# First-layer small TensorE work moved along a handwritten order, in a two-layer encoder kernel

## The chip, the cores and the metric

The kernel runs on one core of a Trainium2 chip. The metric is the device time of one execution, in microseconds (us). TensorE (PE in the profile) multiplies matrices, with its weight loads shown apart as PEld; VectorE (DVE), ScalarE (ACT) and GpSimd (POOL) work beside it, and DMA engines move data between the device memory and the core, at the order of the queues of SP and POOL.

## The reference

The input x has 256 rows of 2048 numbers, all float32. Two layers are computed on it, then a last norm.

```
layer 0:  hn = rmsnorm(x);  q,k,v,u,za,zb = split(hn @ w_in)         (2048 x 6144)
          o_a = chunked_attention(q,k,v, 16 heads x 64) * silu(za)
          y   = gelu(s5(u));  o_b = y * sigmoid(y @ w_glu + b_glu) * silu(zb)
          x   = x + concat(o_a, o_b) @ w_out
layer 1:  q,k,v,z,f = split(rmsnorm(x) @ w_in)                        (2048 x 8208)
          x   = x + (forgetting_attention(q,k,v,f, 16 heads x 128) * silu(z)) @ w_out
out = rmsnorm(x)
```

`s5` is a linear recurrence. For each of 64 channel groups a complex state of 64 numbers follows `x_t = A x_(t-1) + B u_t` over the 256 rows, with A diagonal, and `y_t = Re(C x_t) + D u_t` is read from it.

## The kernel before

**Projections.** All large products go through `project` (L168). A product is cut into column blocks of 512, and a block into chunks: a chunk is one weight tile of 128 x 1024 (512 KB, two blocks of 128 rows). `next_w` (L148) loads the tile into `wr` (4 buffers, issued on SP) and splits it into a high part `wh` on ScalarE and a low part `wl` on VectorE (3 buffers each), so that three matmuls of a reduced format give the product's precision. A chunk is 12 matmuls: two row halves, two blocks, three products of parts. The splits have a priority 3000 instructions ahead of their place.

**A clock of chunks.** The order of TensorE's instructions is the order in which the program writes them (`manual_schedule` for PE, L54); the order on the other engines and the DMA queues comes from a scheduler that simulates the program. Small work on TensorE is put between chunks by hand: `at_chunk(c, task)` queues a generator, `tick` runs after each chunk and resumes what is due, and `yield n` in a task lets n chunks pass. So the text below names a place by the number of chunks ahead of it: u is chunks 0 to 15, za of the first half 16 to 23, then q, k, v, and again za, q, k, v of the second half to 79, zb 80 to 95, the output product of the attention branch `oa0` to `oa3` 96 to 111, GLU 112 to 119, the output product of the other branch `oe0` to `oe3` 120 to 135; layer 1 follows. The host lays the weights in the same order (`_lay`, L1032), since `next_w` takes tile after tile.

**The recurrence (mixer B)** is cut into steps of 8 rows. Its parts, as tasks:
- `setup_task` (L722) prepares powers of A from chunk 3 on, `tables(e, ...)` (L343) then works for one of 8 sets of 8 groups: DVE makes `w1` and `mx`; after GAPS[e] chunks TensorE transposes `w1` (pm, L389) and multiplies `bb` and `mx` to lag tables (pk, L395), which go to device memory as `k_d` (four writes on SP, L402). Then it spawns the next set's `tables`, and at chunk READY[e], at the earliest two chunks on, multiplies u by the table (pv, L414); two chunks later it transposes the result (pvt, L425), and ScalarE copies it into `X`.
- `u_in` (L434) loads u back from device memory in another layout (`un`, L439), spreads it with four ScalarE copies (L445) and transposes it on TensorE (pu, L454) into `uT`, the operand of pv and of the lag products.
- `s5_tail` (L641) is spawned by the last set's pk. It loads the lag tables T0 to T6 with eight DMAs each on POOL's queue (`load_T`, L629) into space that the tables' working tiles have left, into 7 buffers; multiplies u by them (`products`, pyi, L656), one set of 16 small matmuls per table, and after each set loads T7 (after the first) or one of the tiles `mo` into the freed buffer. `scan_task` (L473) runs the recurrence over 30 steps of four DVE instructions. At chunk S5_OUT the second products (py) read `X` and `mo`. Then `yn` goes to device memory, is transposed to `yT` (pyt, L690), the operand of GLU, and read back as `y`, which POOL multiplies into `zb` (L707).

**Attention of layer 0.** `pair` (L577) loads the bias tile `bt` (SP), sets a corner of it on POOL, transposes q and k of two heads (pqk), one chunk later computes scores (psc), and four chunks later transposes the probabilities; `mixes` multiply them by v. The list at L750 says at which chunk each starts.

**GLU** (L780) writes `ob`; `glu_out` transposes it two chunks after each half (po_b, L558), and ScalarE and DVE write the parts `bTh`, `bTl`, the operands of `oe`. In layer 1 `forget` (L823) computes the log gates `lf` on DVE, and TensorE sums them (pc, L875) six chunks later.

Of the kernel before, what the change touches and what calls it, by code (L numbers as in the profile page):

```python
# [11 lines left out]
AF = mybir.ActivationFunctionType  # L12
# [7 lines left out]
D = 2048  # L20
# [7 lines left out]
G, GC, PS5 = 64, 16, 64  # L28
# [8 lines left out]
MAGIC = 12582912.0  # L37
PI_F = 3.1415925
SPLIT_AHEAD = 3000
SCAN_SLOW, S5_OUT = 78, 94  # L40


@with_exitstack
def trunk(ctx: ExitStack, tc: tile.TileContext, a, out: bass.AP):
# [74 lines left out]
    def at_chunk(c, task):  # L119

        seq[0] += 1
        queue.append((c, seq[0], task))
        if not busy:
            run_due()
# [18 lines left out]
        run_due()  # L143


    wpos = [0]

    def next_w(split=None, dst=None):  # L148
        i = wpos[0]
        wpos[0] += 1  # L150
        raw = wp.tile([P, CK * NT], F32, name=f"wr_{i}", tag="wr", bufs=4)
        if dst:
            wh, wl = dst
        else:
            wh = wp.tile([P, CK * NT], F32R, name=f"wh_{i}", tag="wh", bufs=3)
            wl = wp.tile([P, CK * NT], F32R, name=f"wl_{i}", tag="wl", bufs=3)
        step = NT if split else CK * NT
        for o in range(0, CK * NT, step):
            c = slice(o, o + step)
            nc.sync.dma_start(raw[:, c], a["w"][i][:, c])  # L160
            if split:
                split(o // NT)
            with tc.high_priority(offset=SPLIT_AHEAD):
                nc.scalar.activation(wh[:, c], raw[:, c], AF.Copy)  # L164
                nc.vector.tensor_tensor(wl[:, c], raw[:, c], wh[:, c].bitcast(F32), op=ALU.subtract)  # L165
        return wh, wl

# [259 lines left out]
            nc.scalar.copy(X[:, 1:, w, e * 8:e * 8 + 8],  # L427
                           pt[:, w].rearrange("p k (g n) -> p n (k g)", n=NCH))

    GAPS, READY = (9, 6, 6, 6, 6, 6, 7, 7), (24, 0, 0, 0, 0, 0, 0, 0)  # L430
    uT = s5b.tile([P, NGQ, P], F32, name="uT")
    un = X = None

    def u_in():  # L434

        nonlocal un, X
        un = res.tile([P, TC, G * GC // 4], F32, name="un", tag="X")
        for g4 in range(4):
            nc.sync.dma_start(un[32 * g4:32 * g4 + 32],  # L439
                              u_d[:, g4 * 256:(g4 + 1) * 256].rearrange("(n j) f -> n j f", j=TC))  # L440
        un4s = []

        def spread(b):
            un4 = s5b.tile([P, 4, TC, GC], F32, name=f"un4_{b}", tag="vs", bufs=2)
            nc.scalar.copy(un4, un[:, ::-1, b * 64:(b + 1) * 64].rearrange("p j (k c) -> p k j c", c=GC))  # L445
            un4s.append(un4)

        spread(0)
        spread(1)
        yield 3  # L450
        for b in range(4):
            pu = ps_s.tile([P, 4, P], F32, name=f"pu_{b}", tag="s")
            for k in range(4):
                nc.tensor.transpose(pu[:, k, :], un4s[b][:, k].rearrange("p j c -> p (j c)"), ident)  # L454
            nc.scalar.copy(uT[:, b * 4:b * 4 + 4, :], pu)
            if b < 2:
                spread(b + 2)
            if b == 1:
                yield 1
        X = res.tile([P, NCH + 1, 2, G], F32, name="X", tag="X")  # L460
        nc.gpsimd.memset(X[:, 0], 0.0)
# [103 lines left out]
    class Half:  # L565
# [11 lines left out]
        def pair(self, hp):  # L577

            hf = self.hf
            h0 = hf * 8 + hp * 2  # L580
            bt = at.tile([P, 2, L], F32, name=f"bt_{hf}_{hp}", tag="bt")
            nc.sync.dma_start(bt, bass.AP(rbx.tensor, rbx.offset + h0 * 384, [[1, P], [384, 2], [1, L]]))
            nc.gpsimd.memset(bt[0:64, :, 0:64], NEG)
            pqk = ps_s.tile([P, 2, L], F32, name=f"pqk_{hf}_{hp}", tag="s")
            for w, src in ((0, self.q), (1, self.k)):
                for t in range(2):
                    nc.tensor.transpose(pqk[:, w, t * P:(t + 1) * P], src[:, t, hp * P:(hp + 1) * P], ident)
            qkT = at.tile([P, 2, L], F32, name=f"qkT_{hf}_{hp}", tag="qkT")
            nc.scalar.copy(qkT, pqk)
            yield 1  # L590
            pscs = scores(qkT[:, 0, :], qkT[:, 1, :], [slice(0, 64), slice(64, 128)], [f"a{h0}", f"a{h0 + 1}"])
            lgs = [probs(at, pscs[hh], bt[:, hh, P - 1::-1], bt[:, hh, ::-1], f"a{h0 + hh}", scaled=True)
                   for hh in range(2)]
            yield 4
            for hh in range(2):
                self.work.append(turn_probs(at, lgs[hh], f"a{h0 + hh}", scaled=True))
# [44 lines left out]
    def s5_tail():  # L641
# [18 lines left out]
        tabs, mos = [load_T(e) for e in range(7)], []  # L660
        yield 5
        at_chunk(clock[0], scan_task())
        for e in range(8):
            pi_ = products(e, "pyi", lambda gq, g4: uT[:, gq, 32 * g4:32 * g4 + 32], tabs[e])
            nc.scalar.copy(y_of(e), pi_)
            if e == 0:
                tabs.append(load_T(7))
            else:
                mos.append(load_mo(e - 1))
            if e % 2:  # L670
                yield 2 if e < 5 else 4
        yield S5_OUT - clock[0]
        for e in range(8):
            py = products(e, "py", lambda gq, g4: X[:, 0:NCH, 0, gq * 4 + g4], mos[e])
            V.tensor_tensor(y_of(e), py, y_of(e), op=ALU.add)
# [38 lines left out]
    def load_xas(*ns):  # L714
        for n in ns:
            load_xa(n)
        yield None
# [29 lines left out]
    project(xTh, xTl, 16, "u1", u1_out, pre)  # L747
    at_chunk(clock[0], u_in())

    for c, task in ((41, a0.pair(0)), (45, a0.pair(1)), (49, a0.mixes(0)), (49, a0.pair(2)), (52, a0.mixes(1)),  # L750
                    (53, a0.pair(3)), (56, a0.mixes(2)), (60, a0.mixes(3)),
                    (73, a1.pair(0)), (77, a1.pair(1)), (81, a1.mixes(0)), (81, a1.pair(2)), (84, a1.mixes(1)),
                    (85, a1.pair(3)), (88, a1.mixes(2)), (92, a1.mixes(3)), (93, load_xas(0, 1, 2)), (96, load_xas(3))):
        at_chunk(c, task)
    zb = []
    a0.zaT = gate_T(0)
# [10 lines left out]
        project(xTh, xTl, 16, f"zb{n}", silu(z_))  # L767


    for n in range(4):  # L770
        project(aTh, aTl, 8, f"oa{n}",
                lambda t, acc: V.tensor_tensor(xa[n][:, t, :], acc, xa[n][:, t, :], op=ALU.add))


    def glu_out(n, ob):
# [4 lines left out]
    for n in range(2):  # L780
# [9 lines left out]
        project(yT[:, 0], yT[:, 1], 8, f"glu{n}", evac)  # L790
        at_chunk(clock[0], glu_out(n, ob))

    x = res.tile([P, 2, D], F32, name="xr", tag="X")
    x1Th = actp.tile([P, 16, L], F32R, name="x1Th", tag="ah")
    x1Tl = actp.tile([P, 16, L], F32R, name="x1Tl", tag="al")
# [27 lines left out]
    def forget():  # L823
# [45 lines left out]
        nc.vector.tensor_tensor(fe, fe, lf2, op=ALU.mult)  # L869
        nc.vector.scalar_tensor_tensor(fl, fe, -1.0, fl, op0=ALU.add, op1=ALU.add)  # L870
        nc.vector.scalar_tensor_tensor(lf2, fx2, 0.0, fl, op0=ALU.min, op1=ALU.subtract)
        yield 6
        pc = ps_s.tile([P, 2, CH], F32, name="pc", tag="s")
        U = tri[:, P:2 * P]
        nc.tensor.matmul(pc[:, 0, :], U, lf[:, 0, :], start=True, stop=True)  # L875
# [156 lines left out]
def _lay(inputs):  # L1032
    import numpy as np

    f = {k: np.asarray(v) for k, v in inputs.items()}

    def tiles(w, n0, n1):

        w = w[:, n0 * NT:n1 * NT]
        K, N = w.shape  # L1040
        w = w.reshape(K // (CK * P), CK, P, N // NT, NT).transpose(3, 0, 2, 1, 4)
        return w.reshape(-1, P, CK * NT)

    we, wo = f["w_in_even"][0], f["w_in_odd"][0]
    q, k, v, u, za, zb = 0, 2, 4, 6, 8, 10
    order = [u, u + 1, za, q, k, v, za + 1, q + 1, k + 1, v + 1, zb, zb + 1]
    parts = [tiles(we, n, n + 1) for n in order]
    wout = f["w_out_even"][0]
    parts += [tiles(wout[:D // 2], 0, 4), tiles(f["w_glu"][0], 0, 2), tiles(wout[D // 2:], 0, 4)]
    for g in range(4):  # L1050
        parts += [tiles(wo, n, n + 1) for n in (g, 4 + g, 8 + g, 12 + g)]
    parts.append(tiles(f["w_out_odd"][0], 0, 4))

    perm = np.array([(s % 4) * NGQ + s // 4 for s in range(G)])

    def lanes(re, im):
        return np.concatenate([re, im], 0)

    bre, bim = (f[n][0].transpose(1, 0, 2)[:, perm] for n in ("s5_b_re", "s5_b_im"))
    cre, cim = (f[n][0].transpose(2, 0, 1)[:, perm] for n in ("s5_c_re", "s5_c_im"))  # L1060
    bc = np.stack([lanes(bre, bim), lanes(bim, bre), lanes(cre, cim), lanes(cim, cre)], 2)
    d = f["s5_d"][0].reshape(4, NGQ, GC).transpose(0, 2, 1)
    dpad = np.zeros((4, 32, NGQ), d.dtype)
    dpad[:, :GC] = d
    rb = f["rel_bias"][0]
    ext = np.concatenate([rb[:, 1:], np.repeat(rb[:, 256:], 128, 1)], 1)
    return {
        "x": f["x"][0],
        "xT": f["x"][0].T.reshape(16, P, L).transpose(1, 0, 2),
        "w": np.concatenate(parts, 0),  # L1070
        "wf": wo[:, 4 * D:].reshape(16, P, CH).transpose(1, 0, 2).reshape(P, 16 * CH),
        "gE": f["norm_even_g"][0].reshape(16, P).T,
        "gO": f["norm_odd_g"][0].reshape(16, P).T,
        "gF": f["final_norm_g"].reshape(1, D),
        "rbx": ext,
        "bglu": f["b_glu"],
        "bf": f["b_forget"],
        "s5lr": f["s5_lambda_re"][0][perm].T,
        "s5li": f["s5_lambda_im"][0][perm].T,
        "s5dt": f["s5_log_dt"][0][perm].reshape(1, G),  # L1080
        "s5d": dpad.reshape(P, NGQ),
        "s5bc": bc,
    }
# [22 lines left out]
```

## Time and profile before

| what | us |
|---|---|
| median of 3 runs (lowest to highest) | 977.43 (976.41 to 978.26) |
| the profiled execution | 977.11 |
| its span, first to last instruction | 975.4 |
| TensorE busy | 935.1 (96%) |
| VectorE busy | 581.9 (60%) |
| ScalarE busy | 513.5 (53%) |
| GpSimd busy | 104.7 (11%) |
| mean granted TensorE clock | 0.985 |

A row of the list of waits names the waiting engine, its tile and line, who ended the wait, then the time in all, the number of waits and the longest. A row of the timeline has the start and the length of an instruction or of a few alike, the engine, line, operation, out<-in, shapes and count, and in brackets the idle time ahead of it and what ended that. Matmuls overlap in the pipeline, so the time of one is read from start to start, not from its length. A row of windows has the stretch, its length, the busy time and count of PE, PEld, DVE, ACT and POOL, then the granted clock, the DMA share and GB/s. A row of groups has count, then busy time and mean nanoseconds.

### The profile page before, as it was taken

Reading aid. Unit: us, or ns where it says so; the run is one execution under the profiler, and the core shown is the slowest. Engines: PE = TensorE matmul, PEld = TensorE weight load, DVE = VectorE, ACT = ScalarE, POOL = GpSimd, SP = SyncE. Lnnn points to the kernel's source line nnn. Section 1 sums busy time; section 2 is a strip of 40 time slices with the busy share of each in tenths; the row PEclk is TensorE's granted clock in tenths of the full one; section 3 lists DMA queues with packets and bytes.
Section 4 is the critical chain, followed back from the end, with each engine's and each line's share of the span. In section 5 each row is a group of like instructions: output and inputs, shape, how many; then the busy total and the mean of one; then the engine's idle time right before and its main releaser. Section 6 shows DMA issues by size and latency. Waiting matters only on the chain.

```text
span 975.4 us, 13235 instructions
## 1 busy us (share of the span) xinstructions
PE 935.1 (96%) x4814; PEld 759.9 (78%) x4814; DVE 581.9 (60%) x1023; ACT 513.5 (53%) x815; POOL 104.7 (11%) x177
## 2 busy tenths in 40 slices
PE   7969999999689999999999999999999999999996
PEld 5848777777567778887887888888888888888884
DVE  7885777774885446666655545454545454545563
ACT  6636546684246765355544644464446544644451
POOL 2000000001760000200001400040004000200200
PEclk9988999999899999999999999999999999999998
DMA  9885566646988577754556554546564545455562
GB/s 326 288 236 184 189 187 204 203 147 206 198 216 293 177 232 224 230 183 161 173 200 215 174 194 159 195 166 194 171 195 140 199 160 193 153 192 166 192 202 87
DMA packets 68546, 190.43 MB, mean 195 GB/s; under 512 B 7936, under 2 KB 22512, under 8 KB 68096
## 3 DMA queue, kind: packets, MB, share of 16 engines
q1 hardware_dynamic: 65056, 181.07, 56.9%
q0 software_dynamic: 3424, 8.51, 3.8%
q8 instruction: 38, 0.62, 0.3%
q14 instruction: 28, 0.23, 0.1%
HBM read 180.09 MB, written 9.45 MB: 194 GB/s over the span
## 4 chain that ended last, share of the span: by engine, by line
PE 82%; DMA 5%; DVE 5%; issue 3%; ACT 2%; POOL 1%; SPq 1%; POOLq 0%; DVEq 0%; ACTq 0%
PE acc_cq L175 3%; PE acc_cv L177 3%; PE acc_cv L176 3%; PE acc_cz L175 3%; PE acc_cq L177 3%; PE acc_cv L175 3%; PE acc_cq L176 3%; PE acc_cz L177 3%; PE acc_cz L176 3%; PE acc_ck L175 3%; PE acc_ck L176 3%; PE acc_ck L177 3%; PE acc_oo L177 3%; PE acc_oo L175 3%; PE acc_oo L176 3%
## 5 line engine op out<-in xcount | busy, mean ns | idle before, releaser
L165 DVE TENSOR_TENSOR wl<-wr,wh 128x1024 fp32r<-128x1024 f32 (+1 forms) x292 | 360.9, 1236 | 290.2 <-ACT wh L164 289.6
L164 ACT ACTIVATE wh<-wr 128x1024 fp32r<-128x1024 f32 (+1 forms) x292 | 309.7, 1061 | 341.3 <-PE acc_cz L177 46.7
L175 PE MATMUL acc_cv<-wh,x1Th 128*128 128x512 f32 x128 | 51.3, 400 | 0.0
L175 PE MATMUL acc_cq<-wh,x1Th 128*128 128x512 f32 x128 | 50.6, 395 | 0.0
L175 PE MATMUL acc_cz<-wh,x1Th 128*128 128x512 f32 x128 | 50.2, 392 | 0.0
L177 PE MATMUL acc_cv<-wh,x1Tl 128*128 128x512 f32 x128 | 50.0, 390 | 0.0
L175 PE MATMUL acc_ck<-wh,x1Th 128*128 128x512 f32 x128 | 49.9, 390 | 0.0
L176 PE MATMUL acc_cv<-wl,x1Th 128*128 128x512 f32 x128 | 49.9, 390 | 0.0
L177 PE MATMUL acc_cq<-wh,x1Tl 128*128 128x512 f32 x128 | 49.9, 390 | 0.0
L176 PE MATMUL acc_cq<-wl,x1Th 128*128 128x512 f32 x128 | 49.8, 389 | 0.0
L177 PE MATMUL acc_cz<-wh,x1Tl 128*128 128x512 f32 x128 | 49.8, 389 | 0.0
L177 PE MATMUL acc_ck<-wh,x1Tl 128*128 128x512 f32 x128 | 49.8, 389 | 0.0
L176 PE MATMUL acc_ck<-wl,x1Th 128*128 128x512 f32 x128 | 49.8, 389 | 0.0
L176 PE MATMUL acc_cz<-wl,x1Th 128*128 128x512 f32 x128 | 49.8, 389 | 0.0
L910 POOL TENSOR_SCALAR cbt<-ckb,cum 128x128 f32<-128x128 f32 x16 | 13.5, 844 | 309.6 <-DVE mx_c L527 265.4
L175 PE MATMUL acc_oo<-wh,oTh 128*128 128x512 f32 x108 | 42.2, 391 | 0.0
L177 PE MATMUL acc_oo<-wh,oTl 128*128 128x512 f32 x108 | 42.0, 389 | 0.0
L176 PE MATMUL acc_oo<-wl,oTh 128*128 128x512 f32 x108 | 42.0, 389 | 0.0
L633 POOL DMA_DIRECT2D T<-k_d x64 | 33.5, 532 | 41.8 <-DMA k_d<-ks 32.9
L175 PE MATMUL acc_u<-wh,xTh 128*128 128x512 f32 x64 | 26.0, 407 | 6.1 <-ACT wh L164 6.1
L175 PEld LDWEIGHTS acc_ck<-wh,x1Th 128*128 128x128 f32 x128 | 24.0, 188 | 5.4 <-issue 0.4
L177 PEld LDWEIGHTS acc_cq<-wh,x1Tl 128*128 128x128 f32 x128 | 24.0, 188 | 5.1
(407 smaller groups left out, 2084.4 us busy)
## 6 DMA issues: line engine op xcount, KB each, us to landing
wr<-in_w_dram SPq DMA_DIRECT2D x295, 512.0 KB, 3.4
m_d<-mx SPq DMA_DIRECT2D x8, 512.0 KB, 5.4
T<-k_d POOLq DMA_DIRECT2D x64, 64.0 KB, 4.7
mo<-m_d POOLq DMA_DIRECT2D x8, 512.0 KB, 8.2
bt<-in_rbx_dram SPq DMA_DIRECT2D x8, 256.0 KB, 6.2
bc<-in_s5bc_dram SPq DMA_DIRECT2D x8, 256.0 KB, 4.0
xt<-in_x_dram SPq DMA_DIRECT2D x2, 1024.0 KB, 7.8
xa<-in_x_dram SPq DMA_DIRECT2D x4, 512.0 KB, 5.7
```

What stands on the lines that cost most here:

```text
L164: nc.scalar.activation(wh[:, c], raw[:, c], AF.Copy)
L165: nc.vector.tensor_tensor(wl[:, c], raw[:, c], wh[:, c].bitcast(F32), op=ALU.subtract)
L175: nc.tensor.matmul(acc[t], sh, wh[:, c], start=kb == 0, stop=False)
L176: nc.tensor.matmul(acc[t], sh, wl[:, c], start=False, stop=False)
L177: nc.tensor.matmul(acc[t], sl, wh[:, c], start=False, stop=kb == nkb - 1)
L633: nc.gpsimd.dma_start(tt_[j * GC:(j + 1) * GC], k_d[e, :, :, GC * (j + 1):GC * (j + 1) + P])
L910: W.tensor_scalar(bt[:, 0, :], self.ckb[:, hh, 0:P], cum[:, 0, h:h + 1], None, op0=ALU.add)
```

## The change

No computation changes; instructions and the order of weight tiles move.

- The first table's pm and pk come 12 chunks after its DVE work was started instead of 9 (chunk 22 instead of 19), pv of it at chunk 28 instead of 24; the gaps of the last two tables are 6 instead of 7, so the last pm and pk come at chunk 64 instead of 63.
- `u_in` still issues the load of `un` at chunk 16, but spreads at 23 instead of 16 and transposes at 25 and 26 instead of 19 and 20. Each spread copy is tied behind the last `wh` split that the program has written by then (`issue_after` orders instructions of one engine).
- The lag products come one table at a time at chunks 71, 74, ... 92, instead of two at 68, 70, 72 and 76. The scan starts at 69 instead of 68 and changes its pace at 79 instead of 78; the second products start at 95 instead of 94.
- A pair's `bt` load and its memset are written two chunks ahead of its transposes; these stay at their chunks.
- GLU is computed ahead of `oa3` instead of behind it: chunks 108 to 115, with `oa3` at 116 to 119.
- In layer 1 pc comes seven chunks after the gates' DVE work instead of six.

```diff
-SCAN_SLOW, S5_OUT = 78, 94
+SCAN_SLOW, S5_OUT = 79, 95
...
-                nc.scalar.activation(wh[:, c], raw[:, c], AF.Copy)
+                last_split[:] = [nc.scalar.activation(wh[:, c], raw[:, c], AF.Copy)]
...
-    GAPS, READY = (9, 6, 6, 6, 6, 6, 7, 7), (24, 0, 0, 0, 0, 0, 0, 0)
+    GAPS, READY = (12, 6, 6, 6, 6, 6, 6, 6), (28, 0, 0, 0, 0, 0, 0, 0)
...
-            nc.scalar.copy(un4, un[:, ::-1, b * 64:(b + 1) * 64].rearrange("p j (k c) -> p k j c", c=GC))
+            with tc.issue_after(last_split[0].ins):
+                nc.scalar.copy(un4, un[:, ::-1, b * 64:(b + 1) * 64].rearrange("p j (k c) -> p k j c", c=GC))
             un4s.append(un4)
 
+        yield 7
         spread(0)
         spread(1)
-        yield 3
+        yield 2
...
             nc.gpsimd.memset(bt[0:64, :, 0:64], NEG)
+            yield 2
             pqk = ps_s.tile([P, 2, L], F32, name=f"pqk_{hf}_{hp}", tag="s")
...
         yield 5
         at_chunk(clock[0], scan_task())
+        yield 2
         for e in range(8):
...
-            if e % 2:
-                yield 2 if e < 5 else 4
-        yield S5_OUT - clock[0]
+            yield 3 if e < 7 else S5_OUT - clock[0]
...
-    for c, task in ((41, a0.pair(0)), (45, a0.pair(1)), (49, a0.mixes(0)), (49, a0.pair(2)), (52, a0.mixes(1)),
-                    (53, a0.pair(3)), (56, a0.mixes(2)), (60, a0.mixes(3)),
-                    (73, a1.pair(0)), (77, a1.pair(1)), (81, a1.mixes(0)), (81, a1.pair(2)), (84, a1.mixes(1)),
-                    (85, a1.pair(3)), (88, a1.mixes(2)), (92, a1.mixes(3)), (93, load_xas(0, 1, 2)), (96, load_xas(3))):
+    for c, task in ((39, a0.pair(0)), (43, a0.pair(1)), (49, a0.mixes(0)), (47, a0.pair(2)), (52, a0.mixes(1)),
+                    (51, a0.pair(3)), (56, a0.mixes(2)), (60, a0.mixes(3)),
+                    (71, a1.pair(0)), (75, a1.pair(1)), (81, a1.mixes(0)), (79, a1.pair(2)), (84, a1.mixes(1)),
+                    (83, a1.pair(3)), (88, a1.mixes(2)), (92, a1.mixes(3)), (93, load_xas(0, 1, 2)), (96, load_xas(3))):
...
-    for n in range(4):
+    def out_a(n):
         project(aTh, aTl, 8, f"oa{n}",
                 lambda t, acc: V.tensor_tensor(xa[n][:, t, :], acc, xa[n][:, t, :], op=ALU.add))
+
+    for n in range(3):
+        out_a(n)
...
         at_chunk(clock[0], glu_out(n, ob))
 
+    out_a(3)
...
-        yield 6
+        yield 7
         pc = ps_s.tile([P, 2, CH], F32, name="pc", tag="s")
...
-    parts += [tiles(wout[:D // 2], 0, 4), tiles(f["w_glu"][0], 0, 2), tiles(wout[D // 2:], 0, 4)]
+    parts += [tiles(wout[:D // 2], 0, 3), tiles(f["w_glu"][0], 0, 2), tiles(wout[:D // 2], 3, 4),
+              tiles(wout[D // 2:], 0, 4)]
```

More of the change, by code (lines that the diff above doesn't have):

```diff
@@ L143, in tick @@
         run_due()
-    wpos = [0]
+    wpos, last_split = [0], []
     def next_w(split=None, dst=None):
```

## The prediction, made before the changed kernel was run

> **What bounds the kernel now.** I read the list of waits on TensorE first, then TensorE's instructions in time around each long wait, then the other engines and DMA there.
>
> ```profile
> span 975.4 us, 13235 instructions
> ```
>
> ```profile
> PE pyi L656 <- DMA T<-k_d: 11.0, 3, 6.5
> ...
> PE pu L454 <- ACT un L445: 4.9, 1, 4.9
> PE pk L395 <- DVE mx L380: 4.0, 1, 4.0
> PE pc L875 <- DVE lf L871: 0.8, 1, 0.8
> ...
> PE acc_oe L177 <- DVE bTl L561: 0.6, 1, 0.6
> PE acc_oe L175 <- ACT bTh L560: 0.6, 1, 0.6
> ```
>
> The profiled execution took 977.1 us, 1.7 beyond its span; the median of the three runs is 977.4, so a sum made on the one holds for the other within 0.3. TensorE is the bound. These six waits add up to 21.9 us, and all belong to small work that stands in TensorE's handwritten order before its operands are there. The price of a place is more than its wait, because work behind a long wait ran at a lower granted clock. So I measure each place from start to start, and subtract what the same work takes at full clock.
>
> ```profile
> 59.61 0.39 PE L175 MATMUL acc_za<-wh,xTh 128*128 128x512 f32 x1
> ...
> 62.33 1.03 PE L389 MATMUL pm<-ident,w 128*128 128x128 f32 x8
> 67.38 1.08 PE L395 MATMUL pk<-mx,bb 128*32 128x128 f32 x16 [4.02 <-DVE mx L380]
> 73.41 1.97 PE L454 MATMUL pu<-ident,un 128*128 128x128 f32 x8 [4.95 <-ACT un L445]
> ...
> 79.94 1.03 PE L454 MATMUL pu<-ident,un 128*128 128x128 f32 x8
> 80.73 0.47 PE L175 MATMUL acc_za<-wh,xTh 128*128 128x512 f32 x1
> ...
> 96.16 1.04 PE L389 MATMUL pm<-ident,w 128*128 128x128 f32 x8
> 97.12 0.64 PE L395 MATMUL pk<-mx,bb 128*32 128x128 f32 x16
> 97.70 0.50 PE L175 MATMUL acc_q<-wh,xTh 128*128 128x512 f32 x1
> ```
>
> **Place 1, chunk 19.** A chunk takes 2.72 us (59.61 to 62.33). From 62.33 to 80.73 are 18.40 us, in which stand pm (0.96, from 96.16 to 97.12), pk (0.58, to 97.70), two groups of pu (0.79 each, 79.94 to 80.73) and one chunk: 5.84. Lost: 12.6.
>
> ```profile
> 250.07 0.65 PE L656 MATMUL pyi<-T,uT 128*32 128x128 f32 x16
> 257.19 1.08 PE L656 MATMUL pyi<-T,uT 128*32 128x128 f32 x16 [6.47 <-DMA T<-k_d]
> ...
> 277.17 0.85 PE L656 MATMUL pyi<-T,uT 128*32 128x128 f32 x16 [3.73 <-DMA T<-k_d]
> ...
> 285.46 0.49 PE L516 MATMUL psc_a<-qkT 64*128 64x128 f32 x4
> ...
> 286.32 0.50 PE L175 MATMUL acc_v<-wh,xTh 128*128 128x512 f32 x1
> ```
>
> **Place 2, chunks 68 to 73.** From 250.07 to 286.32 are 36.25 us: six lag products (0.58 each, like pk, the same sixteen small matmuls), six chunks (16.32), four transposes of a pair (0.44, half of a group of eight) and its scores (0.86): 21.1. Lost: 15.1.
>
> ```profile
> 436.95 0.40 PE L175 MATMUL acc_oe<-wh,bTh 128*128 128x512 f32 x1
> ...
> 439.76 1.03 PE L558 MATMUL po_b<-ident,ob 128*128 128x128 f32 x8
> ...
> 445.31 0.40 PE L175 MATMUL acc_oe<-wh,bTh 128*128 128x512 f32 x1
> ```
>
> **Place 3, chunk 122.** 5.55 us from po_b to the next chunk but one, less a chunk of this stage (2.81, from 436.95) and eight transposes (0.88): 1.9 lost. **Place 4**, pc: the 0.8 of its wait. Together 12.6 + 15.1 + 1.9 + 0.8 = 30.4.
>
> **The change part by part.** No matmul, copy or DMA is added or taken away; all of it moves.
>
> *First table and u.* pm and pk of table 0 go from chunk 19 to 22, the spread copies of u to 23, pu to 25 and 26, pv to 28.
>
> ```profile
> 66.12 1.21 DVE L380 TENSOR_TENSOR mx<-mx,tm 128x1024 f32<-128x1024 f32 x1
> ```
>
> ```profile
> 62.47 1.30 SPq L439 DMA_DIRECT2D un<-u_d  x2
> ```
>
> ```profile
> 72.74 1.14 ACT L445 COPY un<-un 128x512 f32<-128x512 f32 x2 [8.00 <-DMA un<-u_d]
> ...
> 80.55 1.04 ACT L164 ACTIVATE wh<-wr 128x1024 fp32r<-128x1024 f32 x1
> ```
>
> With nothing at 19, chunk 22 is due at 62.33 + 3 x 2.72 = 70.5; mx is done at 67.3, so pk waits for nothing. Chunk 25 is due at 70.5 + 1.54 + 3 x 2.72 = 80.2; u, issued at 62.47, had landed by 72.74. Before, ScalarE stood 8 us in the spread copy and split no weights again until 80.55. Now issue_after ties the copy behind the split of chunk 22 only. If its static order still has the copy ahead of split 23, that split ends at 72.74 + 1.14 + 1.06 + 1.24 = 76.2 (durations below), while chunk 23 is due at 74.8: 1.4 us. Between 0 and 1.4 I take 0.7. If the copy is late altogether, uT and pv are what comes late next, two and five chunks behind it.
>
> *Tables 1 to 7* follow six chunks apart, the last at 64 instead of 63; tables 1 to 5 kept six before, and the list of waits has none for them; so I take nothing. On SP table 0's k_d writes move back with pk; the weight loads behind them have the lead worked out below: nothing.
>
> *Lag products.* One table per three chunks, from 71, instead of two per two to four from 68.
>
> ```profile
> 241.41 5.82 POOL L633 DMA_DIRECT2D T<-k_d  x11 [32.93 <-DMA k_d<-ks]
> ```
>
> POOL starts the table loads when the last k_d write has landed, so their start goes with pk of table 7. The first product stood 5 chunks behind it and now stands 7. T0 was there in time at 250.07, 8.7 us after POOL's first issue, so it now has over 5.4 us to spare. T1 ended the wait at 257.19, 7.1 us later; T5 20.0 us after that, 5.0 a table. The products now ask for one in at least 3 x 2.72 + 0.58 = 8.7. The waits go. What comes late next is the weights, because TensorE no longer pauses while the tables load:
>
> ```profile
> 62.00:75.00 13.00, 4.04 (x35) 3.19 (x34) 8.36 (x9) 4.04 (x8) 0.00 (x0) 0.65 0.99 262
> 245.00:257.00 12.00, 5.61 (x40) 4.17 (x38) 9.64 (x29) 3.07 (x6) 8.24 (x17) 0.86 1.06 212
> ...
> 290.00:320.00 30.00, 30.00 (x180) 23.32 (x179) 14.12 (x36) 21.52 (x53) 1.45 (x4) 1.00 0.80 291
> ```
>
> ```profile
> L165 DVE TENSOR_TENSOR wl<-wr,wh 128x1024 fp32r<-128x1024 f32 (+1 forms) x292 | 360.9, 1236 | 290.2 <-ACT wh L164 289.6
> L164 ACT ACTIVATE wh<-wr 128x1024 fp32r<-128x1024 f32 (+1 forms) x292 | 309.7, 1061 | 341.3 <-PE acc_cz L177 46.7
> ```
>
> ```profile
> wr<-in_w_dram SPq DMA_DIRECT2D x295, 512.0 KB, 3.4
> ```
>
> The last columns are granted clock (1.00 in the stretch without long waits, 0.65 and 0.86 in those with), DMA share (full from 245 to 257) and GB/s. There 212 GB/s moved; a table (524 kB in 7.1 us) took 74 of it and left 138 for weights, 3.8 us a chunk. A chunk of this stage lasts about 3.2 us with its small work. The tables need 8.7 + 7 x 7.1 = 58 us. A weight tile is asked for six chunks ahead (4 raw buffers, 3 split ones), less two splits of 1.06 + 1.24 and a landing of 3.4: 6 x 3.2 - 4.6 - 3.4 = 11.2 us of lead, an estimate. In 58 us 15.3 chunks land, worth 49.0; with the lead that covers the time: 0. At equal shares of the 212, 106 GB/s and 4.9 us a chunk, 11.8 land, worth 37.9: 58 - 37.9 - 11.2 = 8.9 us of waiting. Between 0 and 8.9 I take 1.0, close to the row. DMA: Bandwidth & Descriptors of the Trainium skill says, under Queues, rings and completion order, that each DMA engine takes turns among the queues with work, a packet at a time; by that rule the sum would go toward the 8.9, while the row at 245 shows the weights with more than half.
>
> On POOL, T7 and the mo loads now wait for products three chunks apart; behind them stand the bt memsets of two pairs, which the edit, like the bt loads on SP, puts two chunks ahead of their transposes: nothing, while that slack holds. Pair transposes stay where they were.
>
> *Scan and second products.* They move by one chunk.
>
> ```profile
> L468 DVE TENSOR_TENSOR st<-e,X x30: 285/292/294, 249.1 to 285.1; 128x128 f32<-128x128 f32 x30
> ```
>
> The scan ran in TensorE's pauses: 36 us for 29 steps with splits between, so at most 37 us in all. Without scan DVE is busy 14.12 of 30 us at TensorE's full pace (290 to 320), 47%. That leaves 1.7 us a chunk, so the scan needs 22 chunks from 69: done at 91, due at 95. For splits that stand behind a scan step I take 0.5; the lower end is 0, the upper 22 x 0.29 = 6.4, nearly all under three split buffers.
>
> *GLU ahead of oa3.* po_b of GLU 1 and its copies now lie beside oa3, four chunks before oe reads bT: 1.9 gained. GLU is due four chunks after pyt instead of eight:
>
> ```profile
> 384.79 1.75 PE pyt L690 x16
> ```
>
> ```profile
> 387.11 2.48 DVE L698 TENSOR_TENSOR yT<-pyt,yT 128x512 fp32r<-128x512 f32 x4
> ```
>
> ```profile
> 391.63 5.89 POOL L707 TENSOR_TENSOR zb<-zb,y 128x1024 f32<-128x1024 f32 x2 [35.42 <-DMA y<-y_d]
> ```
>
> yT is ready 4.8 us after pyt starts, four chunks are 10.9; zb is ready after 12.7, and used after eight chunks, 21.8. Nothing is late. *pc* one chunk later: 0.8 gained.
>
> Sum: 977.1 - 30.4 + 0.7 + 1.0 + 0.5 = 948.9, so **949**.
>
> **Rivals.** (a) *Weights starve behind the tables*, at equal shares: 948.9 - 1.0 + 8.9 = 957. For: DMA share 1.06 at 245. Against: 138 of 212 GB/s went to weights. (b) *u still holds ScalarE* and drags uT copies and the splits of two chunks: up to 1.4 for each of three, so 953. For: the 8 us in the copy. Against: seven microseconds between 72.74 and 80.2. (c) *The change does not do what it says*: only TensorE's order is written by hand, the scheduler orders the rest; if it starts table loads later by what the products were moved, the 15.1 stay: 964. Against: their start hangs on k_d alone. (d) *Slower than before*: the starvation of (a) with weights nearly shut out. It has to cost over 32 us, 58 - 11.2 - 3.2 n > 32, so fewer than five weight chunks landing in 58 us, over 12 us each; place: chunks 70 to 85; time 980. Against: about three landed in the 12 us from 245 (138 GB/s). (e) The gains fall short in several places to no change, 977.
>
> **Chances.** Forecast 0.60 (945.5 to 952.5), (a) 0.19, (b) 0.07, (c) 0.08, (d) 0.04, (e) 0.02. Faster by over 0.2%, about what a measurement of this kernel can tell, is 0.94, same 0.02, slower 0.04. The range takes in forecast, (a) and (b): the low end is all 30.4 gained, 946.7, less the runs' spread of about 1; the high end is (a) plus the larger half of the u cost, 958, plus the spread: 945.5 to 959.5. It leaves 0.14 out.
>
> **What would show it.** Right: no wait of pk, pu or pyi above 0.3 us, PEclk 1.00 from 20 us on, no wait of oe on bT, the scan's last step before chunk 95. Wrong: TensorE waiting for wl or wh behind late wr between chunks 70 and 85 (a); the spread copy ahead of split 23 on ScalarE with a wait after it (b); pyi still waiting for T (c); py waiting for X, or glu for yT, which would add a term that I set at nothing.

## The result: less than half of the forecast gain

The changed kernel takes 966.57 us (median of 4 runs, 965.94 to 967.27), the kernel before, run beside it, 977.85. The ratio is 0.9886, with a 95% interval of 0.9869 to 0.9903: a gain of some 11 us, where the forecast had 28 and its range ended at 959.5. The profiled execution has a span of 965.6 us, 9.8 below the span before, at a mean granted clock of 0.990 (0.985 before).

TensorE's list of waits in the profile after (engine, tile, line, who ended the wait; us in all, times, the longest):

```profile
PE acc_u L175 <- ACT wh L164: 6.0, 1, 6.0
PE pp_a L547 <- ACT lg_a L539: 5.8, 1, 5.8
PE pu L456 <- ACT un L446: 5.1, 1, 5.1
PE acc_q L175 <- ACT za L500: 2.2, 1, 2.2
PE acc_u L176 <- DVE wl L165: 1.3, 2, 0.7
PE acc_za L176 <- DVE wl L165: 0.8, 1, 0.8
PE acc_za L175 <- ACT wh L164: 0.7, 1, 0.7
```

All waits that the change aimed at are gone: pyi, pk, pc and both of acc_oe. The first row is the kernel's start and was there before. In the rows behind it, pp_a, acc_q and the two of acc_za are new, and pu has stayed at about 5 us, seven chunks later (26 instead of 19). So I applied the forecast's own measure, start to start of TensorE's matmuls less the same work at full clock, to every chunk of both traces (2.72 us a chunk, small groups as in the prediction; small work counts with the chunk ahead of it):

| lost TensorE time, us, at chunks | 0-15 | 16-30 | 31-50 | 51-58 | 59-66 | 67-80 | 81-95 | 96-111 | 112-130 | later |
|---|---|---|---|---|---|---|---|---|---|---|
| before | 4.2 | 13.8 | 4.3 | 1.8 | 0.8 | 16.5 | 3.2 | 0.7 | 3.4 | 7.0 |
| after | 4.6 | 10.6 | 2.1 | 5.5 | 0.9 | 1.6 | 11.5 | 2.0 | 1.2 | 5.9 |

The differences add up to the 9.8 us of the spans. The lag products' place, 67 to 80, gave back 14.9 us, as forecast. But 16 to 30 kept 10.6 of 13.8, and two stages lost time that they hadn't lost before: 51 to 58 (3.7 more) and 81 to 95 (8.3 more).

**Chunks 25 and 26.** Rows of the timeline after, of ScalarE, SP's queue and TensorE in order of time (start, length; in brackets the idle time ahead and what ended it):

```profile
73.92 1.14 ACT L446 COPY un<-un 128x512 f32<-128x512 f32 x2 [5.52 <-DMA un<-u_d]
...
82.13 2.52 SPq L402 DMA_DIRECT2D k_d<-ks  x4
84.69 1.00 SPq L340 DMA_DIRECT2D bc<-in_s5bc_dram  x1
...
89.32 0.40 ACT L356 ACTIVATE bc<-bc,nsgn 128x128 f32<-128x128 f32 x1 [6.27 <-DMA bc<-in_s5bc_dram]
...
91.71 0.59 ACT L457 COPY uT<-pu 128x512 f32<-128x512 f32 x1
92.19 0.64 ACT L446 COPY un<-un 128x512 f32<-128x512 f32 x1
...
92.88 2.12 PE L456 MATMUL pu<-ident,un 128*128 128x128 f32 x8 [5.15 <-ACT un L446]
```

`bc` is the input of table 2, which the program turns to at chunk 28. Its load stands on SP behind the four k_d writes of table 0, so it could not be issued before 84.69. The scheduler put the scaling of `bc` on ScalarE ahead of the uT copies and of the last two spread copies. ScalarE stood at it for 6.27 us, and TensorE's pu 5.15. Chunks 25 and 26 lose 7.1 us of the 10.6. The first row has a price of its own: the next weight splits stood behind the spread copy, TensorE waited for them 0.66 and 0.77 us at chunk 23 (the rows of acc_za above), and chunks 22 and 23 lose 2.1 us.

**Chunk 56.** The same picture with the input of table 7, which the program turns to at chunk 58: k_d, then `bc` on SP, VectorE and ScalarE at the first operations that read it, the probabilities and the evacuation of za behind them.

```profile
190.99 3.20 SPq L402 DMA_DIRECT2D k_d<-ks  x4
194.23 0.58 SPq L340 DMA_DIRECT2D bc<-in_s5bc_dram  x1
...
198.24 0.40 ACT L356 ACTIVATE bc<-bc,nsgn 128x128 f32<-128x128 f32 x1 [1.83 <-DMA bc<-in_s5bc_dram]
198.24 0.42 DVE L351 TENSOR_TENSOR bb<-bc,cr 128x256 f32<-128x256 f32 x1 [2.16 <-DMA bc<-in_s5bc_dram]
...
207.25 0.50 PE L175 MATMUL acc_q<-wh,xTh 128*128 128x512 f32 x1 [2.20 <-ACT za L500]
```

**Chunk 86.** Rows of POOL, TensorE and VectorE:

```profile
295.97 0.60 PE L520 MATMUL psc_a<-qkT 64*128 64x256 f32 x4
...
296.44 1.20 POOL L636 DMA_DIRECT2D T<-k_d  x2 [1.58 <-DMA T<-k_d]
...
300.80 0.22 POOL L585 MEMSET bt<- 64x128 f32 x1
...
311.25 1.22 DVE L165 TENSOR_TENSOR wl<-wr,wh 128x1024 fp32r<-128x1024 f32 x1 [1.98 <-ACT wh L164]
312.39 0.28 DVE L527 CUSTOM_DVE_ANT_0 lg_a<-psc_a,bt 128x128 f32<-128x128 f32 x1
...
315.91 1.78 PE L547 MATMUL pp_a<-ident,lg_a 128*128 128x128 f32 x6 [5.83 <-ACT lg_a L539]
```

The scores were there at 296.6. The corner of `bt` was set at 301.0, because the memset stands on POOL behind the last table loads and an `mo` load. Yet VectorE took up the scores (L527) at 312.39 only, behind a weight split at 311.25 that had waited 1.98 us for ScalarE's part of it. By this reading it isn't the memset's own time that cost, but the place in VectorE's static order that came with it; that was the theory to test.

### The profile page after: what moved, and what is told of

It reads as the page before. It is cut to its first block, busy times and chain, and to the rows that moved or that the text cites. A ratio compares the mean times of both kernels' runs of the same rounds, so it can differ in the third digit from the quotient of the medians.

```text
span 965.6 us, 13241 instructions
## 1 busy us (share of the span) xinstructions
PE 933.5 (97%) x4814; PEld 758.8 (79%) x4814; DVE 579.4 (60%) x1023; ACT 517.0 (54%) x817; POOL 104.4 (11%) x177
## 4 chain that ended last, share of the span: by engine, by line
PE 85%; DVE 4%; DMA 3%; ACT 3%; issue 3%; SPq 1%; POOL 0%; POOLq 0%; DVEq 0%; ACTq 0%
PE acc_cq L175 3%; PE acc_cv L177 3%; PE acc_ck L175 3%; PE acc_cq L177 3%; PE acc_cv L176 3%; PE acc_cz L177 3%; PE acc_cv L175 3%; PE acc_cq L176 3%; PE acc_cz L175 3%; PE acc_ck L177 3%; PE acc_ck L176 3%; PE acc_cz L176 3%; PE acc_oo L177 3%; PE acc_oo L175 3%; PE acc_oo L176 3%
## 5 line engine op out<-in xcount | busy, mean ns | idle before, releaser
L916 POOL TENSOR_SCALAR cbt<-ckb,cum 128x128 f32<-128x128 f32 x16 | 13.8, 861 | 308.8 <-DVE mx_c L529 261.9
L175 PE MATMUL acc_q<-wh,xTh 128*128 128x512 f32 x64 | 26.8, 418 | 2.3 <-ACT za L500 2.2
```

The costliest lines, as they stand in the source:

```text
L175: nc.tensor.matmul(acc[t], sh, wh[:, c], start=kb == 0, stop=False)
L916: W.tensor_scalar(bt[:, 0, :], self.ckb[:, hh, 0:P], cum[:, 0, h:h + 1], None, op0=ALU.add)
```

## The experiments

The theory: the forecast's gain was there, and was given back where an engine that works in order met an operation that waited for a DMA (the `bc` scalings) or one placed too late because of such a wait (the probabilities behind the memset). The rivals: u's landing itself holds ScalarE; weights or VectorE's time are short; lost time moves wherever the order changes. Times are medians, ratios to runs of the kernel before on the same chip.

**1. The memset on VectorE** (the kernel after, and this):

```diff
-            nc.gpsimd.memset(bt[0:64, :, 0:64], NEG)
+            nc.vector.memset(bt[0:64, :, 0:64], NEG)
```

> The changed kernel, with the memset of a pair's bias corner on VectorE instead of GpSimd. Theory (queue order): the 5.8 us wait of pp_a at chunk 86 comes from the memset standing on GpSimd's queue behind the table and mo loads, because of which the scheduler put the pair's VectorE work behind the split of chunk 88; then the wait goes and 8.8 us with it, 966.6 to about 958. Rival (VectorE is too full with the scan, or weights are late): pp_a still waits some 5 us, 966.

Measured: 970.45 us, 0.9918 (0.9896 to 0.9939). The wait of pp_a is gone, but the time is no shorter than that of the changed kernel (0.9886, with an interval that touches this one). Two waits in the list and VectorE's timeline in this run:

```profile
PE poa L615 <- ACT v L491: 5.1, 1, 5.1
PE acc_v L176 <- DVE wl L165: 4.6, 1, 4.6
```

```profile
279.48 0.17 DVE L585 MEMSET bt<- 64x128 f32 x1 [7.62 <-DMA bt<-in_rbx_dram]
...
300.10 0.17 DVE L585 MEMSET bt<- 64x128 f32 x1 [7.79 <-DMA bt<-in_rbx_dram]
```

The memset reads nothing, but writes into a tile that the load writes first, so VectorE now stood 7.6 and 7.8 us for the load, with splits behind it. The wait went from POOL's queue to VectorE's.

**2. `bc` issued ahead of the k_d writes:**

```diff
+        if e < 6:
+            bcs.append(load_bc(e + 2))
         for g4 in range(4):
             nc.sync.dma_start(k_d[e, :, g4::4, :], ks[32 * g4:32 * g4 + GC])
...
-            if e < 6:
-                bcs.append(load_bc(e + 2))
```

> The changed kernel, with the load of set e+2's b and c tile issued ahead of the k_d writes of set e instead of behind them. Theory (the bc load on SP holds ScalarE): ScalarE no longer stands 6.3 us in the bc scaling at 83 to 89 us, the 5.1 us wait of pu goes and its half-clock stretch, about 7 us; the ScalarE hold at 198 us that leads to the 2.2 us wait of acc_q goes too, about 4 more: 966.6 to about 956. Rival (u itself is what comes late): pu waits as before at chunk 26, 966.

Measured: 967.30 us, 0.9891 (0.9871 to 0.9911). ScalarE in this run:

```profile
75.79 0.39 ACT L356 ACTIVATE bc<-bc,nsgn 128x128 f32<-128x128 f32 x1
...
89.45 0.40 ACT L356 ACTIVATE bc<-bc,nsgn 128x128 f32<-128x128 f32 x1 [4.76 <-DMA bc<-in_s5bc_dram]
```

Table 2's scaling now ran at 75.79 without a wait, and the scheduler put that of table 3 in its place, ahead of the uT copies: pu waited 4.3 us. The place at chunk 56 was mended (1.4 us lost at 51 to 58 instead of 5.5), and 31 to 50 lost 6.4 instead of 2.1. An earlier load only moves the head on by one table.

**3. Both edits:**

> The changed kernel with both edits of e1 and e2. If the two causes are separate and complete, the gains add up: 966.6 - 8.8 - 11 = about 947, which is close to the blind forecast of 949. If one wait only hides the other, less than 15 us in all, above 951.

Measured: 968.14 us, 0.9897 (0.9878 to 0.9916). Waits of both kinds stayed: poa on v 4.8, acc_v on wl 3.6, pu on un 3.8.

**4. The GLU part alone, on the kernel before:**

```diff
-    for n in range(4):
+    for n in range(3):
         out_a(n)
...
+    out_a(3)
```

> The kernel before with only GLU computed ahead of oa3 (and the weights in that order). Theory: the two waits of oe on bT (1.2 us) go and 1.9 us in all, 977.9 to about 976.0. Rival (yT or zb late at chunk 108 instead of 112): glu waits, no change or slower, 977.9 or more.

Measured: 975.48 us, 0.9977 (0.9961 to 0.9993). Both waits of acc_oe are gone, and chunks 112 to 130 lose 1.2 us instead of 3.4. The forecast had 1.9 for it.

**5. Table heads kept near their turn** (the kernel after, and this; the first five operations of a table, all that read `bc`, are tied behind the last weight split that the program has written):

```diff
+                last_split[:] = [nc.scalar.activation(wh[:, c], raw[:, c], AF.Copy),
+                                 nc.vector.tensor_tensor(wl[:, c], raw[:, c], wh[:, c].bitcast(F32), op=ALU.subtract)]
...
+        with ExitStack() as held:
+            for ins in last_split:
+                held.enter_context(tc.issue_after(ins.ins))
+            V.tensor_tensor(bb, bc[:, :, 0:2, :],
```

> The kernel after the change, with the first five operations of each table (three on VectorE, two on ScalarE, all of which read the bc load) tied behind the last weight split given out, so that neither engine can meet a table's head before that table's turn. Theory (the wait moved to chunk 25 because ScalarE stands 6.3 us at the next table's bc scaling, whose load was queued on SP behind the k_d writes; the place at chunk 56 is the same thing): the wait of pu falls from 5.1 to under 1 us, the wait of acc_q from 2.2 to under 0.7, chunks 16 to 30 lose at most 5 us instead of 10.6, chunks 51 to 58 at most 2 instead of 5.5; the wait of pp_a on ScalarE (5.8) stays; time 957 to 960. Rival (u itself holds ScalarE, by its landing at 73.9 us, and bc only stands behind it): pu still waits 4 us or more, time 964 to 967.

Measured: 960.82 us, 0.9822 (0.9808 to 0.9837). The place at chunk 56 is gone (acc_q 0.3 us, 1.9 lost at 51 to 58). At chunk 25 only part of the wait went:

```profile
PE pu L459 <- ACT un L449: 3.9, 1, 3.9
```

```profile
86.14 0.40 ACT L359 ACTIVATE bc<-bc,nsgn 128x128 f32<-128x128 f32 x1 [4.68 <-DMA bc<-in_s5bc_dram]
```

By the numbers this lies between theory and rival: pu waits nearly the rival's 4. ScalarE still stands at `bc` ahead of the uT copies, since the split that the head is tied to runs some chunks ahead of TensorE. Run 10 ties it behind the copies themselves.

**6. The corner set before the load:**

```diff
-            nc.sync.dma_start(bt, bass.AP(rbx.tensor, rbx.offset + h0 * 384, [[1, P], [384, 2], [1, L]]))
-            nc.gpsimd.memset(bt[0:64, :, 0:64], NEG)
+            nc.vector.memset(bt[0:64, :, 0:64], NEG)
+            nc.sync.dma_start(bt[64:], bass.AP(rbx.tensor, rbx.offset + h0 * 384 + 64, [[1, 64], [384, 2], [1, L]]))
+            nc.sync.dma_start(bt[0:64, :, 64:], bass.AP(rbx.tensor, rbx.offset + h0 * 384 + 64, [[1, 64], [384, 2], [1, L - 64]]))
```

> The kernel after the change, with the bias tile's masked corner set by VectorE before its load instead of by GpSimd after it, and the load cut in two so that it leaves the corner alone: the masking now waits for no DMA and stands behind no table load. Theory (the wait of pp_a at chunk 86 came because the masking stood on GpSimd behind the table loads, and the waits of the run with the masking on VectorE came because VectorE then stood 7.6 and 7.8 us at it for the bias load): the wait of pp_a falls from 5.8 to under 0.5, no wait of poa on v or of acc_v on wl above 0.7 comes in its place, chunks 67 to 95 lose at most 5 us instead of 13.1; time 957 to 960. Rival (the stage is short of something else, weights or VectorE's time beside the scan, and the lost time only moves again): over 9 us still lost in chunks 67 to 95, time 964 to 968.

Measured: 955.06 us, 0.9767 (0.9753 to 0.9782), beyond what the theory asked. No memset waits for a load any more, and VectorE takes up the pair's scores at once. From its summary of the memset's line (durations in ns, then first and last start) and the timeline, where the scores of this pair start at 293.39:

```profile
L584 DVE MEMSET bt<- x8: 165/165/165, 1.5 to 281.7; 64x128 f32 x8
```

```profile
293.39 0.60 PE L520 MATMUL psc_a<-qkT 64*128 64x256 f32 x4
...
295.16 0.28 DVE L527 CUSTOM_DVE_ANT_0 lg_a<-psc_a,bt 128x128 f32<-128x128 f32 x1
...
307.35 0.82 PE L547 MATMUL pp_a<-ident,lg_a 128*128 128x128 f32 x6
```

pp_a has no wait, chunks 81 to 95 lose 2.9 us instead of 11.5, and 67 to 80 stay at 1.6. The same loads, scan and splits stand in this stage, so the rival (weights or VectorE's time short) falls.

**7. Runs 5 and 6 together:**

> The kernel after the change with both edits together. Theory (the forecast's gain was there, and what ate it is these two orders): 966.6 - 6 to 9 - 8 = 948 to 953, near the forecast of 949; remaining TensorE waits only the 6.0 at the start and some under 1 us. Rival (lost time moves with every change of the order): 958 or more, with a wait of 3 us or more at a new place.

Measured: 952.85 us, 0.9742 (0.9728 to 0.9757). The time is in the range of the theory, but the two gains do not add up: by the ratios run 5 gained 6.3 us over the changed kernel, run 6 11.6 and this run 14.1. Part of them is the same place: chunks 16 to 30 lose 8.0 us in run 5, 8.1 in run 6, which left the table heads alone, and 7.3 here, instead of 10.6. One wait over 1 us is left besides the start:

```profile
PE pu L459 <- ACT un L449: 3.6, 2, 3.2
```

**8. The lag products alone, on the kernel before** (the products start at chunk 71 as in the change; the scan stays at 68 and S5_OUT at 94):

```diff
+        yield 3
         for e in range(8):
...
-            if e % 2:
-                yield 2 if e < 5 else 4
-        yield S5_OUT - clock[0]
+            yield 3 if e < 7 else S5_OUT - clock[0]
```

> The kernel before with the lag products alone moved: one table per three chunks from chunk 71, second products at 94; u, first table, GLU as before. Theory (the lag part's own gain is the 15.1 us of its place, less what the masking behind the later table loads costs): no pyi wait, chunks 67 to 80 lose under 4 us instead of 16.5, a wait of pp_a or poa of 4 us or more comes between chunks 75 and 95, time 965 to 973. Forecast's reading (nothing comes back): 964 or less. Rival (loads later by what the products were moved): pyi still waits, 975 or more.

Measured: 970.65 us, 0.9930 (0.9913 to 0.9946). No wait of pyi; chunks 67 to 80 lose 1.7 us instead of 16.5, and 81 to 95 lose 11.0 instead of 3.2, with the known wait:

```profile
PE pp_a L545 <- ACT lg_a L537: 5.8, 1, 5.8
```

So this part alone carries the place at chunk 86: 14.8 gained, 7.8 given back. The pairs' own places were not touched here: the later table loads and `mo` loads on POOL, ahead of the memset, are enough.

**9. The u part alone, on the kernel before** (GAPS, READY, the yields of `u_in` and `issue_after`; the lag products keep their chunks, one chunk nearer to the table loads):

```diff
-    GAPS, READY = (9, 6, 6, 6, 6, 6, 7, 7), (24, 0, 0, 0, 0, 0, 0, 0)
+    GAPS, READY = (12, 6, 6, 6, 6, 6, 6, 6), (28, 0, 0, 0, 0, 0, 0, 0)
...
-        yield 5
+        yield 4
         at_chunk(clock[0], scan_task())
```

> The kernel before with the u part alone: first table and u three chunks later, tables six apart; lag products, pairs, GLU and pc as before. Theory (the part takes the waits of chunk 19 away and brings one of pu at chunk 25 or 26, behind a bc load on ScalarE, so that 3 us of its 12.6 stay gained): no wait of pk, pu waits 3 us or more, pyi's waits of about 11 stay, time 973 to 978. The forecast's reading (12.6 less 0.7): 967 or less.

Measured: 987.17 us, 1.0100 (1.0078 to 1.0122): slower, and 9 us above my own expectation. The list of waits:

```profile
PE pyi L658 <- DMA T<-k_d: 14.4, 4, 7.1
PE acc_v L176 <- DVE wl L165: 8.0, 1, 8.0
...
PE pu L456 <- ACT un L446: 4.7, 1, 4.7
```

In the places that the theory named it was as expected: pk gone, pu 4.7, 9.6 lost at 16 to 30 (4.2 gained), 5.2 at 51 to 58. The miss is behind it. The lag products stand one chunk closer to the loads and wait 14.4 us, and VectorE's order puts more than ten scan steps in a row ahead of one weight split; 67 to 80 lose 30.2. That the order of the scan made the 8.0 is read from the trace; no run tested it. The parts are no sum: the u part needs the later lag products.

**10. Run 7, with the heads tied behind the uT copies too:**

```diff
+            last_u[:] = [nc.scalar.copy(uT[:, b * 4:b * 4 + 4, :], pu)]
...
-            for ins in last_split:
+            for ins in last_split + last_u:
```

> The run with both edits (table heads in order, corner set before the load) and, besides, the heads of tables 2 and later tied behind the last uT copy out of pu. Theory (in that run pu still waited 3.2 us because ScalarE stood 4.0 us at table 2's bc scaling ahead of the uT copies: the split it was tied to runs three chunks ahead of TensorE): pu waits under 1 us, chunks 16 to 30 lose at most 4.5 us instead of 7.3, time 947 to 950. Rival (u's landing holds it, through pm, ks and the pu copies): pu waits 2 us or more, 952 to 953.

Measured: 948.00 us (947.87 to 950.74), 0.9710 (0.9690 to 0.9730). This beats both kernels, and run 7 by 3 us by the ratios. TensorE's whole list of waits, and ScalarE in the place:

```profile
PE acc_u L175 <- ACT wh L164: 6.8, 2, 6.1
PE acc_u L176 <- DVE wl L165: 1.1, 2, 0.8
PE acc_glu L175 <- DVE xa L778: 0.6, 1, 0.6
PE acc_q L175 <- ACT za L503: 0.5, 2, 0.3
```

```profile
72.70 1.14 ACT L449 COPY un<-un 128x512 f32<-128x512 f32 x2 [5.05 <-DMA un<-u_d]
...
84.32 0.60 ACT L460 COPY uT<-pu 128x512 f32<-128x512 f32 x1
...
88.84 0.41 ACT L359 ACTIVATE bc<-bc,nsgn 128x128 f32<-128x128 f32 x1
```

The uT copy comes at 84.32 instead of 91.71, the head of table 2 after it, without a wait. Note the first row: ScalarE still stands 5.05 us for u, and TensorE has no wait. So the hold of u need not cost anything; in the kernel after, where the copy came 1.2 us later and TensorE reached chunk 22 1.0 us sooner, it cost 2.1 us at chunks 22 and 23. Chunks 16 to 30 lose 1.5 us.

**11. The spread copies, pu and pv two chunks later again** (the kernel after, and this alone):

```diff
-    GAPS, READY = (12, 6, 6, 6, 6, 6, 6, 6), (28, 0, 0, 0, 0, 0, 0, 0)
+    GAPS, READY = (12, 6, 6, 6, 6, 6, 6, 6), (30, 0, 0, 0, 0, 0, 0, 0)
...
-        yield 7
+        yield 9
         spread(0)
```

> The kernel after the change with the spread copies of u, pu and pv two chunks later again, nothing else. It tests the first link of the chain: u holds ScalarE until it lands, so ks, k_d's writes on SP and the bc load behind them come late, and ScalarE then stands at bc. Theory: the 5.5 us in the spread copy fall below 2, bc lands 3 us or more sooner, pu waits under 1, chunks 16 to 30 lose at most 6 us instead of 10.6, acc_q's and pp_a's waits stay; time 960 to 963. Rival (bc is late for reasons of its own): pu waits 3 us or more, 965 to 967.

Measured: 958.97 us, 0.9822 (0.9797 to 0.9846). The wait of pu is gone and 16 to 30 lose 5.1 us, but not for the reason that I gave:

```profile
71.17 1.06 ACT L164 ACTIVATE wh<-wr 128x1024 fp32r<-128x1024 f32 x1 [3.90 <-DMA wr<-in_w_dram]
...
83.28 0.58 SPq L340 DMA_DIRECT2D bc<-in_s5bc_dram  x1
...
87.15 0.40 ACT L356 ACTIVATE bc<-bc,nsgn 128x128 f32<-128x128 f32 x1 [3.78 <-DMA bc<-in_s5bc_dram]
```

Without u in its way ScalarE stood for weights, k_d was written at 80.66 instead of 82.13, and `bc` was issued only 1.4 us and used only 2.2 us sooner (3 expected). So u's hold is no more than a small part of why `bc` is late. It follows k_d, and k_d follows the copies out of pk: VectorE's, the later one, ended 7.6 us behind pk here and 9.2 in the kernel after. pu was saved because its own place moved behind the landing of `bc`; ScalarE still stood at the scaling, and acc_q now waits 2.25 us for za at chunk 24.

**12. Run 10 with the later spread:**

> Table heads in order and behind the uT copies, corner set before the load, and the spread copies two chunks later: every link that I know of removed. Theory: the remaining waits are the 6.0 at the start and some under 1 us, chunks 16 to 30 lose at most 4 us, time 945 to 949, at or below the forecast. Rival (with the heads behind the uT copies the later spread brings nothing, or table 1's or 2's mx and pk come late): within 1 us of the run without it, or above.

Measured: 948.95 us, 0.9714 (0.9695 to 0.9734), within 1 us of run 10, as the rival had it: with the heads behind the uT copies the later spread has nothing left to remove. It brings a wait of acc_q for za of 1.65 us at chunk 24, which the theory did not have.

## Why the prediction was wrong

The forecast gained 28.2 us in its own sum, and the trace shows 9.8. By its steps:

| step of the forecast | forecast, us | in the trace, us |
|---|---|---|
| place 1, first table and u (chunks 16-30) | 12.6 - 0.7 | 3.2 |
| "the weight loads behind" k_d, and tables six apart: nothing (51-58) | 0 | -3.7 |
| place 2, lag products (67-80) | 15.1 - 1.0 - 0.5 | 14.9 |
| bt memsets behind T7 and mo: nothing (81-95) | 0 | -8.3 |
| place 3, GLU (112-130) | 1.9 | 2.2 |
| place 4, pc (later) | 0.8 | 1.1 |
| elsewhere (0-15, 31-50, 59-66, 96-111) | 0 | 0.4 |

**What was right.** The measure of the places, and that work would start on time once its operands were there: with the two orders mended, run 10 came to 948.0 where the forecast said 949.0. By stages run 10 gained 12.3 us at chunks 16 to 30, 14.9 at 67 to 80 and 2.2 at 112 to 130, against 11.9, 13.6 and 1.9. That the total comes within 1 us is in part luck: run 10 also gained 2.1 us at 31 to 50, which the forecast didn't have, and lost some 3.6 at 0 to 15 and 96 to 111. Rivals (a) and (d), weights starving behind the tables, did not come: a window row of the profile after (stretch; length; busy time and count of PE, PEld, DVE, ACT, POOL; granted clock, DMA share, GB/s) over the table loads:

```profile
257.00:298.00 41.00, 41.00 (x259) 31.54 (x252) 38.10 (x124) 26.78 (x53) 23.39 (x45) 1.00 1.05 234
```

TensorE is busy throughout at full clock, with the DMA engines full, at 234 GB/s. The sum by equal shares asked for 8.9 us; no wait for weights shows in this stage. The 44 table loads of 64 KB that POOL issued in these 41 us make some 70 of the 234 GB/s, an estimate from its rows. The Trainium skill's page DMA: Bandwidth & Descriptors (section Queues, rings and completion order) says that each DMA engine takes turns among the queues with work, a packet at a time; this trace does not show equal shares in bytes. The scan ended before py needed it (the last step started at 306.7, the first py at 349.6), with no wait for it.

**The first step that failed** is the sentence "On SP table 0's k_d writes move back with pk; the weight loads behind them have the lead worked out below: nothing." The weight loads had it. But the next table's `bc` load stands behind the same writes on the same queue, and went back with them by three chunks, while the uT copies and za's evacuation, which the scheduler ordered behind the `bc` scalings, came at about the same chunks. Price: 7.1 us at chunks 25 and 26, most of the 8.7 by which place 1 fell short, and 3.7 at chunk 56. Runs 5 and 10 showed it by taking the scalings out of the way: the load was issued only 2.6 and 1.6 us sooner (82.10 and 83.07 instead of 84.69), and run 5 freed chunk 56, run 10 chunks 25 and 26. Rival (b) named ScalarE, but for u, and at 4 us. Its sign came, the spread copy ahead of the next split with a wait after it, and cost 2.1 us at chunks 22 and 23 where the forecast took 0.7 between 0 and 1.4; the long wait of pu was not its work, as runs 10 and 11 showed.

**The second step that failed** is "nothing, while that slack holds" for the memsets. The slack didn't hold. POOL's 64 table loads lasted 55.0 us (242.69 to 297.64) instead of 42.4 before (241.41 to 283.82). Only T7's eight ask for a lag product, the first, which was long done; nearly every pause of POOL between the loads ended when an earlier one landed. An `mo` load behind them then waited 2.01 us for a lag product. So the memset came at 300.80, four us after the scores that it belongs to, and VectorE's order then had the probabilities behind splits until 312.39. The forecast had the number for this: its own 58 us for the tables, counted from 242.7, end near 301, behind the scores at 296.6. Price 8.3. Run 8 showed that the lag part alone brings it, run 6 that it goes once the memset waits for neither POOL's queue nor the load.

The table loads also last 54.3 us in run 8, 52.6 in run 6 and 55.7 in run 10, where TensorE doesn't pause beside them, and 42.0 in run 9, where it does. That the weights moving beside them slow them is read from this and from the full DMA engines; no run isolates it.

Both steps have one form. I asked who waits for the moved work, and took the engines' own orders as given; but the scheduler made them anew, and a place where an engine may stop for a DMA took with it whatever was ordered behind. I gave that no bound in the range, though the profile before has a row for it, between two rows of ScalarE that the prediction shows:

```profile
80.05 0.40 ACT L356 ACTIVATE bc<-bc,nsgn 128x128 f32<-128x128 f32 x1 [3.17 <-DMA bc<-in_s5bc_dram]
```

Before the change, too, ScalarE stood at table 2's scaling, ahead of the last uT copies, and this, not the spread copy alone, kept it from the splits until 80.55.

**What stays open:** the split that came late behind scan steps in run 9; why run 6 gained at chunks 16 to 30; and 2.2 us that chunks 31 to 50 gained and the forecast didn't have. Run 9 shows that the u part brings them (2.2 lost there with it alone, 4.3 before), but not how.

## What to carry to other kernels

When a write or a product is moved, list the *loads* behind it in the same DMA queue, and for each the engine whose next operation waits for it: that engine stops with everything ordered behind. Where such an operation isn't due yet, tie it behind the work that is; where it waits for a DMA only because it writes the same tile, do it before the load on bytes that the load leaves alone. Price a place on a handwritten order as what it loses at most if an engine's order changes around it, and expect parts of a change to be no sum.

## What the runs showed of the hardware

A wait costs more than its length, as in the kernel before. Around the 5.83 us of pp_a the window row of the profile after reads:

```profile
309.00:322.00 13.00, 7.17 (x41) 4.53 (x40) 4.55 (x24) 6.17 (x19) 0.53 (x1) 0.74 0.71 267
```

The granted clock is 0.74 over the stretch, and the place at chunk 86 lost 8.3 us for a wait of 5.83. Run 10, with no single wait over 0.8 us after the start, had a mean clock of 0.997. What I hadn't expected is which of the two loads gave way. While the tables loaded, 235 GB/s moved in the profile after (242.7 to 297.6) and 237 in run 10 (231.5 to 287.2), with a DMA share of 1.03 in both, TensorE at full clock and no wait for weights; in the profile before, with TensorE's pauses, it was 190 at a share of 0.87 (241.4 to 283.8). It was the table loads that took longer, 55.0 and 55.7 us instead of 42.4.
